# A two-layer decoder trunk on one core: high part of the gated block one flush later, weight-form sums spread behind the residual additions, one activation for the layer 1 operand

## The chip, the cores and the metric

The kernel runs on one core of a Trainium2 chip. The metric is the device time of one execution in microseconds, the median of several runs. Its engines are named as in the profile: PE (matmul) with PEld (weight loads), DVE (vector), ACT (activation), POOL (GpSimd) and SP, which only issues DMAs here.

## The reference, cut to what matters

Two request groups, 1024 prompt positions and 64 sample positions, go through two layers with the same weights. Each layer adds a token mixer (layer 0: convolution and attention; layer 1: short convolution and pooling) and then a gated channel mixer to the residual. The change touches the channel mixers of both layers and the step from layer 0 to layer 1.

```
def rms_norm(x, g):   # x * rsqrt(mean(x*x) + EPS) * g
def swiglu(h, w_in, w_out):
    g, u = jnp.split(h @ w_in, 2, axis=-1)
    return (jax.nn.silu(g) * u) @ w_out
...
for layer in range(DEPTH):                       # DEPTH 2, D_MODEL 1024, FFN_DIM 2816
    hn = rms_norm(h, norm_mix_g[layer])
    ...
    h = h + mix
    h = h + swiglu(rms_norm(h, norm_ffn_g[layer]), w_ffn_in[layer], w_ffn_out[layer])
y = rms_norm(h, norm_final_g)
```

All is float32. A product is made of three matmuls on numbers that are split in a high part (rounded for the PE) and a low part (the rest): high by high, high by low, low by high.

## The kernel before, in words

The residual `hb` lies on chip, transposed: 8 tiles of 128 channels, with 1088 columns for the positions. The columns are worked on as group A (`GA`, 512 columns), group B (`GB`, 576 columns, in two pieces of 288) or both (`GT`, pieces of 364). The order in time is: layer 0 mixers; layer 0 channel mixer of A, with attention in the background; of B; layer 1 mixer for both; layer 1 channel mixer of A; of B with the output.

Weights. `seq` lists the weight blocks in the order in which PE uses them. `w_next()` hands out the next and, before that, prepares the block two places on (`w_split`) and issues loads further on (`w_load`, four `stage` buffers, on SP's queue). To prepare a plain block, ACT copies the high part from `stage` to a tile `hl` (L177) and POOL subtracts to get the low part (L179). There are three `hl` buffers.

The channel mixer (`run_ffn`) has 22 hidden blocks f of 128 channels. Two of them make a group q. After the products of group q+1 come the output products of group q: two weight blocks (o = 0, 1), of four output tiles each (`out_block`, six pieces of matmul per tile and 512 columns), each added to the residual by DVE (`added`, L274). I call these eight output tiles of a group the *out section*, and number them 0 to 7. PE writes results to PSUM accumulators; `accs()` has three buffers in the channel mixers, so output tile 3 needs the addition of tile 0 to be done, tile 4 that of tile 1, and so on.

From f = 5 on, in both groups of layer 1 and in group B of layer 0, the two input products of a block are made with seven half-size products in place of eight (`strassen`). Their weights are four *forms* r = 0 to 3 of a block, of two halves each, built from the two staged halves by four subtractions or additions on DVE: three for form 0 (L186, L187, L188, tile `sum`), one for form 2 or 3 (L191). ACT takes the high part of each half (L194), POOL the low part (L195). In `strassen` PE makes X (two products), Y (two), Z (two), W (one); ACT copies a part of Y (L468), which all of the seven DVE additions (L456) need; the second of these frees X's accumulator, which W takes. The three sums for form 0 of the first block of the next group are issued by the `w_next` of o = 0, at the start of the out section, and so stand on DVE ahead of the additions of the out section.

The gated block. `gated` puts a function `fin` on the list `post`: POOL multiplies (L430), ACT copies the high part to `hid` (L431); the low part (DVE, L432) goes to `late`. `flush()` runs what is on `post` and then what was on `late`; it is called in every plain block, behind X in `strassen`, and behind output tile 1.

Within an engine the instructions run in the order of the program. `tc.manual_schedule()` leaves that order as written.

The step to layer 1 (`to_mixer`) is the last out section of layer 0, group B. For each tile n: the addition, squares (ACT L230, POOL L231), ACT makes the high part of the layer 1 operand `x1` (L351) for B and then for A, and DVE the low parts (L354): that of B one tile later, that of A for all eight tiles behind the whole section.

Of the kernel before, what the change touches and what calls it, by code (L numbers as in the profile page):

```python
# [8 lines left out]
F = mybir.dt.float32  # L9
# [20 lines left out]
def f32(ap):  # L30
    return ap.bitcast(F)
# [27 lines left out]
def trunk_kernel(ctx, tc, x_prompt, x_sample, cache_k, cache_v, state_conformer, state_shortconv, state_pool,  # L59
# [106 lines left out]
    sums = {}  # L166

    def w_split(upto):
        while nxt[1] < min(upto, len(seq)):
            i = nxt[1]  # L170
            w_load(need(i + 1))
            a, b, r = seq[i]
            hl = wpool.tile([128, 2, 1024], FR, name="hl", bufs=3)
            lo, hi = slice(0, 512), slice(512, 1024)
            if b is None:
                st = stage.pop(a)
                act.activation(hl[:, 0], st, AF.Copy)  # L177
                for c in (lo, hi):
                    pool.tensor_tensor(hl[:, 1, c], st[:, c], f32(hl[:, 0, c]), op=OP.subtract)  # L179
                hls[i] = hl.rearrange("p s (k n) -> p s k n", k=loads[a][1])  # L180
            else:
                sg, su = stage[a], stage[b]
                if r == 0:
                    sums["a"], sums["b"] = (sums["p"].tile([128, n], F, name=f"sum{n}") for n in (1024, 512))
                    sa, sb = sums["a"], sums["b"]
                    dve.tensor_tensor(sb[:, lo], su[:, lo], su[:, hi], op=OP.add)  # L186
                    dve.tensor_tensor(sa[:, hi], sg[:, lo], su[:, lo], op=OP.subtract)  # L187
                    dve.tensor_tensor(sa[:, lo], sb[:, lo], sg[:, lo], op=OP.subtract)  # L188
                sa, sb = sums["a"], sums["b"]
                if r == 2:  # L190
                    dve.tensor_tensor(sa[:, hi], sg[:, hi], sa[:, lo], op=OP.subtract)  # L191
                src = ((sa[:, lo], sa[:, hi]), (sb[:, lo], sg[:, lo]), (su[:, hi], sg[:, hi]), (sa[:, hi],))[r]
                for c, x in zip((lo, hi), src):
                    act.activation(hl[:, 0, c], x, AF.Copy)  # L194
                    pool.tensor_tensor(hl[:, 1, c], x, f32(hl[:, 0, c]), op=OP.subtract)  # L195
                if r == 3:
# [83 lines left out]
    def flush():  # L280
        todo, low_parts = post[:], late[:]
        post.clear()
        late.clear()
        for f in todo + low_parts:
            f()
# [63 lines left out]
    def prep(g, x, n, gain, squares=False, c0=0):  # L349
        o, i = x[n][:, :, c0:c0 + g.n], hb[:, n, g.cs]  # L350
# [51 lines left out]
    def run_ffn(g, accs, ps, hidp, x, last, sig=False, slot=lambda: None, forms=None):  # L402
# [21 lines left out]
        def gated(f, t, u):  # L424
# [4 lines left out]
            def fin():  # L429
                pool.tensor_tensor(t[:, :n], t[:, :n], u[:, :n], op=OP.mult)  # L430
                act.activation(dst[:, 0], t[:, :n], AF.Copy)  # L431
                late.append(lambda: dve.tensor_tensor(dst[:, 1], t[:, :n], f32(dst[:, 0]), op=OP.subtract))  # L432
# [52 lines left out]
        for q in range(G + 1):  # L485
# [776 lines left out]
    knew = consts.tile([128, 4, NS], F, name="knew")  # L1262
# [52 lines left out]
    def to_mixer(hh):  # L1315
# [9 lines left out]
        for o in range(2):  # L1325
            h = w_next()
            for i in range(4):
# [399 lines left out]
```

## Time and profile before

| | us |
|---|---|
| median of 3 runs (2681.70 to 2682.96) | 2682.24 |
| the profiled execution | 2677.37 |
| its span, first to last instruction | 2675.2 |
| PE busy in it | 2540.1 (95%) |
| POOL, DVE, ACT busy | 1569.5 (59%), 1637.9 (61%), 1084.8 (41%) |

The mean granted TensorE clock is 0.988. Matmul ends in the trace are modelled, so PE's busy time is an upper figure; the gaps between its instructions and what ended them are what is read below. A row of the wait view says: engine, line, what it waited for, the sum in us, how many times, the longest. A row of the timeline says: start and length in us, engine, line, operation, out<-in, shapes, how many in a row, and in brackets the idle time before it and what ended it.

### The profile page before, as it was taken

The page shows a single profiled execution, that of the slowest core. Times are in us where ns is not written, and L with a number is a line of the kernel's source. Part 1 is how long each engine was busy: PE and PEld are TensorE (multiplying, and loading weights), DVE is VectorE, ACT ScalarE, POOL GpSimd, SP SyncE. Part 2 cuts the span into 40 slices and gives each one's busy share as a digit, 9 for nine tenths or more (in the row PEclk, how much of TensorE's full clock was granted, in tenths as well). Part 3 has the DMA queues.
Part 4 walks back from the last instruction along what each step waited for, and adds up shares of the span by engine and source line. Part 5 has one row for each costly group of instructions (what it writes and reads, how often), then busy time and mean ns, then how long its engine had stood idle before and what let it go on. Part 6 is the DMA issues. An engine that isn't in the chain of part 4 may idle for free. (4 is left out here: it accounts for less than half of the span.)

```text
span 2675.2 us, 40716 instructions
## 1 busy us (share of the span) xinstructions
PE 2540.1 (95%) x15627; PEld 2257.4 (84%) x15627; DVE 1637.9 (61%) x2262; ACT 1084.8 (41%) x1814; POOL 1569.5 (59%) x1199
## 2 busy tenths in 40 slices
PE   8989998999999998999999899999999999999998
PEld 6788877887666656999999899998788888999997
DVE  3774776868756634377666633333666676666665
ACT  5436766744343324343333422122333334333333
POOL 6756244444333337478788722234788887677875
PEclk9999999999999999999999999999999999999999
DMA  7332241234445434322332411131232333233232
GB/s 218 114 97 71 62 112 36 71 112 117 142 142 152 119 110 128 89 72 80 95 95 87 128 44 40 42 113 34 87 93 87 90 95 95 67 104 107 85 90 75
DMA packets 346008, 254.06 MB, mean 95 GB/s; under 512 B 22657, under 2 KB 295169, under 8 KB 345800
## 3 DMA queue, kind: packets, MB, share of 16 engines
q1 hardware_dynamic: 345784, 251.46, 32.1%
q8 instruction: 124, 2.03, 0.3%
q14 instruction: 68, 0.56, 0.1%
q10 hardware_dynamic: 32, 0.01, 0.0%
HBM read 233.21 MB, written 18.69 MB: 94 GB/s over the span
## 5 line engine op out<-in xcount | busy, mean ns | idle before, releaser
L179 POOL TENSOR_TENSOR hl<-stage,hl 128x512 fp32r<-128x512 f32 x484 | 667.6, 1405 | 481.5 <-ACT hl L177 323.7
L214 PE MATMUL acc<-x,hl 128*128 128x288 f32 (+1 forms) x3792 | 710.1, 340 | 12.0 <-DVE hb L274 7.4
L214 PEld LDWEIGHTS acc<-x,hl 128*128 128x128 f32 x3792 | 585.0, 190 | 98.7 <-issue 35.3
L214 PE MATMUL acc<-hid,hl 128*128 128x288 f32 (+1 forms) x3072 | 551.0, 335 | 35.3 <-DVE hb L274 23.6
L214 PEld LDWEIGHTS acc<-hid,hl 128*128 128x128 f32 x3072 | 465.1, 190 | 105.8 <-DVE hb L274 35.1
L274 DVE TENSOR_TENSOR hb<-acc,hb 128x512 f32<-128x512 f32 (+2 forms) x376 | 263.6, 717 | 224.2 <-PE acc L214 222.1
L195 POOL TENSOR_TENSOR hl<-sum,hl 128x512 fp32r<-128x512 f32 x204 | 282.8, 1403 | 172.6 <-ACT hl L194 167.1
L452 PE MATMUL acc<-tt,hl 128*128 128x288 f32 (+1 forms) x2448 | 331.6, 291 | 0.6 <-ACT hl L194 0.3
L452 PEld LDWEIGHTS acc<-tt,hl 128*128 128x128 f32 x2448 | 321.0, 189 | 1.9 <-ACT hl L194 0.6
L177 ACT ACTIVATE hl<-stage 128x1024 fp32r<-128x1024 f32 x242 | 252.0, 1052 | 142.7 <-PE acc L214 100.9
L214 PE MATMUL acc<-x1t,hl 128*128 128x364 f32 (+1 forms) x1728 | 293.8, 331 | 7.4 <-DVE x1t L354 4.1
L214 PEld LDWEIGHTS acc<-x1t,hl 128*128 128x128 f32 x1728 | 288.9, 190 | 9.3 <-DVE x1t L354 4.4
L452 PE MATMUL acc<-x,hl 128*128 128x288 f32 (+1 forms) x1836 | 256.9, 292 | 18.0 <-ACT hl L177 12.9
L456 DVE TENSOR_TENSOR tmp<-acc,tmp 128x288 f32<-128x288 f32 (+1 forms) x357 | 146.5, 442 | 202.7 <-ACT tmp L468 157.9
L452 PEld LDWEIGHTS acc<-x,hl 128*128 128x128 f32 x1836 | 243.8, 190 | 20.8 <-ACT hl L177 19.2
L195 POOL TENSOR_TENSOR hl<-stage,hl 128x512 fp32r<-128x512 f32 x153 | 229.7, 1524 | 20.8 <-ACT hl L194 10.5
L270 DVE TENSOR_TENSOR tmp<-acc,rr 128x512 f32<-128x512 f32 (+3 forms) x128 | 89.7, 712 | 204.7 <-PE acc L214 189.2
L194 ACT ACTIVATE hl<-sum 128x512 fp32r<-128x512 f32 x204 | 122.1, 623 | 186.1 <-DVE sum L188 119.1
L431 ACT ACTIVATE hid<-tmp 128x512 fp32r<-128x512 f32 (+1 forms) x88 | 57.9, 657 | 326.6 <-POOL tmp L430 326.5
L231 POOL TENSOR_TENSOR ss<-ss,tmp 128x512 f32<-128x512 f32 (+2 forms) x62 | 105.2, 1696 | 87.8 <-ACT tmp L230 84.4
L430 POOL TENSOR_TENSOR tmp<-tmp 128x512 f32<-128x512 f32 (+1 forms) x88 | 125.7, 1429 | 26.4 <-ACT tmp L416 25.4
L214 PE MATMUL acc<-x1a,hl 128*128 128x512 f32 x480 | 121.3, 406 | 2.5 <-POOL hl L179 1.3
(252 smaller groups left out, 2936.4 us busy)
## 6 DMA issues: line engine op xcount, KB each, us to landing
stage<-in_w_ffn_in_dram SPq DMA_DIRECT2D x176, 512.0 KB
stage<-in_w_ffn_out_dram SPq DMA_DIRECT2D x88, 512.0 KB
stage<-in_w_in_even_dram SPq DMA_DIRECT2D x40, 512.0 KB
kst<-in_cache_k_dram SPq DMA_DIRECT2D x64, 256.0 KB
vst<-in_cache_v_dram SPq DMA_DIRECT2D x64, 256.0 KB
stage<-in_w_out_even_dram SPq DMA_DIRECT2D x16, 512.0 KB
stage<-in_w_in_odd_dram SPq DMA_DIRECT2D x16, 512.0 KB
park<-hb SPq DMA_DIRECT2D x16, 288.0 KB
```

What stands on the lines that cost most here:

```text
L177: act.activation(hl[:, 0], st, AF.Copy)
L179: pool.tensor_tensor(hl[:, 1, c], st[:, c], f32(hl[:, 0, c]), op=OP.subtract)
L194: act.activation(hl[:, 0, c], x, AF.Copy)
L195: pool.tensor_tensor(hl[:, 1, c], x, f32(hl[:, 0, c]), op=OP.subtract)
L214: pe.matmul(acc[:, b, :c1 - c0], w, x[:, xi, c0:c1], start=first and s == 0, stop=last and s == 2)
L231: pool.tensor_tensor(ss[:, g.cs], ss[:, g.cs], t[:, :g.n], op=OP.add)
L270: dve.tensor_tensor(d, a, r, op=OP.mult)
L274: dve.tensor_tensor(d, a, d, op=OP.add)
L430: pool.tensor_tensor(t[:, :n], t[:, :n], u[:, :n], op=OP.mult)
L431: act.activation(dst[:, 0], t[:, :n], AF.Copy)
L452: pe.matmul(acc[:, :w2], h[:, wi, i, k], xk[:, xi], start=k == 0 and s == 0, stop=k == 3 and s == 2)
L456: dve.tensor_tensor(out, acc[:, :w2], x, op=OP.add)
```

## The change

There are four edits:

1. `fin` has only POOL's multiplication; ACT's high part and DVE's low part are both issued one flush later.
2. In the out section `w_next` runs with `thin` set: the three sums of form 0, and with the third its high and low parts (`cut`), go to `parts_`, and one is run behind each of the additions of output tiles 0, 1 and 2.
3. The fourth sum (form 3) gets a tile of its own, `sum_c`, instead of half of the tile `sum`, and the staged weights are given free at form 2 instead of form 3. `knew` moves from the permanent pool to one that ends with the layer 0 channel mixer of A.
4. In `to_mixer` one activation of 1088 columns makes the high part for both groups; the low parts of A for tiles 0 and 1 are made within the section, the other six behind it.

```diff
@@ w_split
+            a, b, r = seq[i]
             w_load(need(i + 1))
-            a, b, r = seq[i]
...
+                if r == 0:
+                    todo = [lambda: dve.tensor_tensor(sb, su[:, lo], su[:, hi], op=OP.add),
+                            lambda: dve.tensor_tensor(sa[:, hi], sg[:, lo], su[:, lo], op=OP.subtract),
+                            lambda cut=cut: (dve.tensor_tensor(sa[:, lo], sb, sg[:, lo], op=OP.subtract),
+                                     cut(src=(sa[:, lo], sa[:, hi])))]
+                    if thin[0]:
+                        parts_.extend(todo)
+                    else:
+                        for f in todo:
+                            f()
+                else:
+                    while parts_:
+                        parts_.pop(0)()
+                    if r == 2:
+                        sums["c"] = sums["p"].tile([128, 512], F, name="sum_c")
+                        dve.tensor_tensor(sums["c"], sg[:, hi], sa[:, lo], op=OP.subtract)
+                    cut(src=(sb, sg[:, lo]) if r == 1 else (su[:, hi], sg[:, hi]) if r == 2 else (sums["c"],))
                 if r == 2:
...
                     stage.pop(a), stage.pop(b)
@@ gated
                 pool.tensor_tensor(t[:, :n], t[:, :n], u[:, :n], op=OP.mult)
-                act.activation(dst[:, 0], t[:, :n], AF.Copy)
-                late.append(lambda: dve.tensor_tensor(dst[:, 1], t[:, :n], f32(dst[:, 0]), op=OP.subtract))
+                late.append(lambda: split(dst, t[:, :n]))
@@ run_ffn, out section
+                    thin[0] = True
                     h = w_next()
+                    thin[0] = False
                     for i in range(4):
                         a = accs()
                         out_block(g, a, h, i, hh)
                         added(g, hb[:, o * 4 + i, g.cs], a)
+                        if parts_:
+                            parts_.pop(0)()
                         if o == 0 and i == 1:
                             flush()
@@ to_mixer
-                prep(GB, x1, n, pc(MIXG + 8 + n), c0=HALF)
+                gain = pc(MIXG + 8 + n)
+                act.activation(x1[n][:, 0], hb[:, n], AF.Copy, scale=gain)
+                for gr in (GB, GA):
+                    lowq.append(lambda gr=gr, n=n, gain=gain: dve.scalar_tensor_tensor(
+                        x1[n][:, 1, gr.cs], hb[:, n, gr.cs], gain, f32(x1[n][:, 0, gr.cs]), op0=OP.mult,
+                        op1=OP.subtract))
+                if n > 1:
+                    behind.append(lowq.pop())
                 low(1)
-                prep(GA, x1, n, pc(MIXG + 8 + n))
-                behind.append(lowq.pop())
```

ACT, layer 1 channel mixer of group A, from the second `strassen` of a group through the out section, before. `hid` is the gated block, `sum` and `stage` the sources of the forms, L468 the copy out of Y, L177 the two output weight blocks, L481 the silu:

```order
L194 ACTIVATE hl<-stage 128x512 x2
L431 ACTIVATE hid<-tmp 128x512
L194 ACTIVATE hl<-sum_18363 128x512
L468 ACTIVATE tmp<-acc 128x256
L177 ACTIVATE hl<-stage 128x1024 x2
L481 ACTIVATE tmp<-tmp 128x512
L194 ACTIVATE hl<-sum_18551 128x512 x2
L431 ACTIVATE hid<-tmp 128x512
```

The same stretch of ACT now, where the split of `hid` is L231, the forms L189, the copy out of Y L479 and the silu L492:

```order
L189 ACTIVATE hl<-stage 128x512 x2
L189 ACTIVATE hl<-sum_c 128x512
L479 ACTIVATE tmp<-acc 128x256
L177 ACTIVATE hl<-stage 128x1024 x2
L492 ACTIVATE tmp<-tmp 128x512
L231 ACTIVATE hid<-tmp 128x512
L189 ACTIVATE hl<-sum_18566 128x512 x2
```

The copy to `hid` that stood between form 2 and form 3 is gone from there; it now stands in the out section, ahead of form 0.

DVE, the same group, from the second block's additions through the out section, before:

```order
L456 TENSOR_TENSOR tmp<-acc,tmp 128x256 x7
L186 TENSOR_TENSOR sum_20586<-stage 128x512
L187 TENSOR_TENSOR sum_20585<-stage 128x512
L188 TENSOR_TENSOR sum_20585<-sum_20586,stage 128x512
L274 TENSOR_TENSOR hb<-acc,hb 128x512 x2
L432 TENSOR_TENSOR hid<-tmp,hid 128x512
L274 TENSOR_TENSOR hb<-acc,hb 128x512 x6
L191 TENSOR_TENSOR sum_20585<-stage,sum_20585 128x512
```

DVE now, with L286 the residual addition, L193 to L195 the three sums, L232 the low part of `hid`:

```order
L467 TENSOR_TENSOR tmp<-acc,tmp 128x256 x7
L286 TENSOR_TENSOR hb<-acc,hb 128x512
L193 TENSOR_TENSOR sum_20613<-stage 128x512
L286 TENSOR_TENSOR hb<-acc,hb 128x512
L194 TENSOR_TENSOR sum_20612<-stage 128x512
L232 TENSOR_TENSOR hid<-tmp,hid 128x512
L286 TENSOR_TENSOR hb<-acc,hb 128x512
L195 TENSOR_TENSOR sum_20612<-sum_20613,stage 128x512
L286 TENSOR_TENSOR hb<-acc,hb 128x512 x5
L207 TENSOR_TENSOR sum_c<-stage,sum_20612 128x512
```

The first addition now comes ahead of all sums; the third comes behind two sums and the low part.

DVE in the step to layer 1, now; `x1t` is the operand, 576 columns are B and 512 are A. Before, each addition from the third on was followed by one low part of B, and all of A's came at the end:

```order
L286 TENSOR_TENSOR hb<-acc,hb 128x576
L1352 SCALAR_TENSOR_TENSOR x1t_15056<-hb,par,x1t_15056 128x576
L286 TENSOR_TENSOR hb<-acc,hb 128x576
L1352 SCALAR_TENSOR_TENSOR x1t_15056<-hb,par,x1t_15056 128x512
L1352 SCALAR_TENSOR_TENSOR x1t_15057<-hb,par,x1t_15057 128x576
L286 TENSOR_TENSOR hb<-acc,hb 128x576
L1352 SCALAR_TENSOR_TENSOR x1t_15057<-hb,par,x1t_15057 128x512
L286 TENSOR_TENSOR hb<-acc,hb 128x576
L1352 SCALAR_TENSOR_TENSOR x1t_15058<-hb,par,x1t_15058 128x576
```

The low part of B for tile 0 now stands ahead of the second addition, and A's first two low parts stand within the section.

More of the change, by code (lines that the diff above doesn't have):

```diff
@@ L164, in need @@
         return max(a, b or 0) + 1
-    sums = {}
+    sums, parts_, thin = {}, [], [False]
     def w_split(upto):
@@ L280, in flush @@
     def flush():
-        todo, low_parts = post[:], late[:]
+        todo = post + late
         post.clear()
         late.clear()
-        for f in todo + low_parts:
+        for f in todo:
             f()
@@ L1261, in trunk_kernel @@
     hidp = hstack.enter_context(tc.tile_pool(name="hid0", bufs=2, side="right"))
[L1262 removed]
+    knew = hstack.enter_context(tc.tile_pool(name="knewp", bufs=1, side="right")).tile([128, 4, NS], F, name="knew")
     act.activation(knew, kall[:, :, SEQ:T], AF.Copy)
```

20 lines of the change are left out of this document (7 added, 13 removed).

## The prediction

> **What bounds the kernel now.** I read the busy shares first, then who PE waits for by stage, then one period of the steady state engine by engine.
>
> ```profile
> PE 2540.1 (95%) x15627; PEld 2257.4 (84%) x15627; DVE 1637.9 (61%) x2262; ACT 1084.8 (41%) x1814; POOL 1569.5 (59%) x1199
> ```
>
> PE is the bound: 2675.2 of span less 2540.1 leaves 135 us in which it stands, and no edit removes a matmul. So the question is which of PE's waits end at what the edits move. The waits of the stretches with forms, in order: layer 1 group A (1926 to 2226 us), layer 0 group B (1205 to 1500), layer 1 group B (2330 to 2620).
>
> ```profile
> PE acc L452 <- ACT hl L177: 12.9, 9, 2.1
> PE acc L214 <- DVE hb L274: 9.9, 8, 1.3
> ```
> ```profile
> PE acc L214 <- DVE hb L274: 3.3, 8, 0.6
> PE acc L452 <- DVE tmp L456: 3.2, 3, 2.1
> ```
> ```profile
> PE acc L214 <- DVE hb L274: 3.3, 6, 0.7
> PE acc L452 <- DVE tmp L456: 1.6, 1, 1.6
> ```
>
> Two kinds of wait recur: one inside `strassen` (L452), one in the out section (L214 for L274). Here is a period of group A in layer 1: PE, then ACT, DVE, POOL.
>
> ```profile
> 2038.29 1.60 PE L452 MATMUL acc<-x,hl 128*128 128x256 f32 x12
> 2041.24 1.66 PE L452 MATMUL acc<-x,hl 128*128 128x256 f32 x12 [1.36 <-ACT hl L177]
> 2042.74 4.42 PE L214 MATMUL acc<-hid,hl 128*128 128x512 f32 x18
> 2048.39 0.97 PE L214 MATMUL acc<-hid,hl 128*128 128x512 f32 x3 [1.24 <-DVE hb L274]
> ```
> ```profile
> 2038.76 0.63 ACT L431 ACTIVATE hid<-tmp 128x512 fp32r<-128x512 f32 x1 [5.34 <-POOL tmp L430]
> 2039.30 0.61 ACT L194 ACTIVATE hl<-sum 128x512 fp32r<-128x512 f32 x1
> 2039.82 0.37 ACT L468 ACTIVATE tmp<-acc 128x256 f32<-128x256 f32 x1
> 2040.08 2.00 ACT L177 ACTIVATE hl<-stage 128x1024 fp32r<-128x1024 f32 x2
> ```
> ```profile
> 2040.21 2.43 DVE L456 TENSOR_TENSOR tmp<-acc,tmp 128x256 f32<-128x256 f32 x6 [6.40 <-ACT tmp L468]
> 2042.94 0.42 DVE L456 TENSOR_TENSOR tmp<-acc,tmp 128x256 f32<-128x256 f32 x1 [0.30 <-PE acc L452]
> 2043.28 1.06 DVE L186 TENSOR_TENSOR sum<-stage 128x512 f32<-128x512 f32 x1
> 2044.27 1.77 DVE L187 TENSOR_TENSOR sum<-stage 128x512 f32<-128x512 f32 x1
> 2045.96 1.78 DVE L188 TENSOR_TENSOR sum<-sum,stage 128x512 f32<-128x512 f32 x1
> 2047.66 1.27 DVE L274 TENSOR_TENSOR hb<-acc,hb 128x512 f32<-128x512 f32 x2
> 2048.86 1.54 DVE L432 TENSOR_TENSOR hid<-tmp,hid 128x512 fp32r<-128x512 f32 x1
> ```
> ```profile
> 2037.43 1.30 POOL L430 TENSOR_TENSOR tmp<-tmp 128x512 f32<-128x512 f32 x1
> 2039.99 1.27 POOL L195 TENSOR_TENSOR hl<-sum,hl 128x512 fp32r<-128x512 f32 x1 [1.26 <-ACT hl L194]
> 2041.26 5.93 POOL L179 TENSOR_TENSOR hl<-stage,hl 128x512 fp32r<-128x512 f32 x4
> ```
>
> ```profile
> ACT hid L431 <- POOL tmp L430: 326.5, 76, 8.2
> ```
>
> The last row is the sum over the run. The first wait of the period: ACT stands 5.34 us for POOL's multiplication, with L194 and L468 queued behind; DVE stands 6.40 us for L468; its second addition frees X's accumulator at about 2041.1, and PE's W, ready at 2039.9 (2038.29 and 1.60), starts at 2041.24. The row names L177, but L177 is itself behind L431 and L468. The second wait: three tiles take PE from 2042.74 to 2047.16; tile 3 needs the addition of tile 0, which stands behind the three sums and ends at 2048.3.
>
> **The change, part by part.** *A, the copy to hid a flush later.* ACT then meets L431 when its product has long been made. L468 can run when Y is done, just before Z's second product starts at 2038.29; two additions of 0.4 us then free X by about 2039.2, before W is wanted. So the whole 1.36 goes. Eight of the nine waits are such: 12.9 less the longest, 2.1, is 10.8 us. The longest of each stretch (2.1, 2.1, 1.6) is at the first `strassen`, where DVE has other work until shortly before:
>
> ```profile
> 2334.73 1.91 DVE L191 TENSOR_TENSOR sum<-stage,sum 128x512 f32<-128x512 f32 x1
> 2337.72 1.54 DVE L456 TENSOR_TENSOR tmp<-acc,tmp 128x288 f32<-128x288 f32 x3 [1.08 <-ACT tmp L468]
> ```
>
> There only DVE's 1.08 of idleness can be saved: 3 x 1.1 = 3.3. The other two waits of layer 0 (3.2 less 2.1) are 1.1. Together 15.2 us; from below 10 (the steady ones, a little short), from above 17.7 (all of 12.9, 3.2 and 1.6). The delayed copy itself costs nothing inside, since `hid` is read a group later. At the three run ends it stands between the product and DVE's low part; at most 3 x 0.63, and I take 0, since by then eight additions lie between.
>
> *B, sums behind additions.* Nothing is removed: three sums, two or three additions and L432 are the same DVE work in another order. Walk it for group A, with W at 2039.9, so tile 0 at 2041.4 and 1.47 us per tile (4.42/3). The addition of tile 0 (0.69) ends at 2043.8. A sum alone and a sum next to POOL:
>
> ```profile
> 2027.35 0.69 DVE L187 TENSOR_TENSOR sum<-stage 128x512 f32<-128x512 f32 x1 [1.19 <-POOL hl L195]
> ```
>
> 0.69 there, 1.77 above, where POOL ran L179. The first sum meets POOL (L179, then L430): 1.77, to 2045.5; addition 1 to 2046.2; if POOL is done, second sum, L432 and addition 2 take 3 x 0.69, to 2048.3. Tile 3 (2045.8) and tile 4 (2047.3) are then free of waiting, and tile 5 starts at 2048.75, after addition 2. If the second sum meets POOL too, addition 2 ends at 2049.4 and tile 5 waits 0.6; if L432 (1.54 above) does as well, about 1.5, more than the 1.24 before. I take 0.2, near zero, for two reasons: form 3's low part no longer waits 1.26 on POOL, so that its four L179 start earlier, and with `sum_c` the 1.19 before L187 goes too, which brings POOL's earlier parts forward. So 9.9 - 8 x 0.2 = 8.3; bounds -2 and 9.9. In group B a tile takes longer:
>
> ```profile
> 2451.28 4.92 PE L214 MATMUL acc<-hid,hl 128*128 128x288 f32 x36
> 2456.71 8.20 PE L214 MATMUL acc<-hid,hl 128*128 128x288 f32 x60 [0.51 <-DVE hb L274]
> ```
>
> ```profile
> 1531.47 0.75 DVE L274 TENSOR_TENSOR hb<-acc,hb 128x576 f32<-128x576 f32 x1
> ```
>
> The tile takes 1.64 (4.92/3) and its addition 0.75, so tile 5 starts 8.2 after tile 0. DVE there: addition 0 ends at 2.6, then at worst two sums of 1.77, an L432 of 1.54 and two additions of 0.75: 9.2; with one contended, 7.3. I take no wait: 3.3 + 3.3 = 6.6; from below 3. B is 14.9 us. The Trainium skill's page "SBUF — State Buffer" (Who interferes with whom) calls the port that DVE and POOL share a lock for a whole instruction, taken by a DVE operation with two SBUF inputs and blocking the other engine's. By that a sum behind a POOL operation would take 0.69 + 1.30, an estimated 2.0, where the trace has 1.77, and a contended second sum would cost tile 5 another 0.2, so 1.6 us of the sum over eight sections. It speaks against sums between additions, in the direction that the rows show; I keep the rows' 1.77.
>
> *C, the layer 1 operand.* ACT, PE and DVE at the step to layer 1:
>
> ```profile
> 1519.72 1.37 ACT L351 ACTIVATE x1t<-hb,par 128x576 fp32r<-128x576 f32 x2
> 1521.00 0.67 ACT L230 ACTIVATE tmp<-hb 128x576 f32<-128x576 f32 x1
> ```
> ```profile
> 1532.37 0.74 PE L214 MATMUL acc<-x1t,hl 128*128 128x364 f32 x3 [2.88 <-DVE hb L274]
> 1537.17 2.18 PE L214 MATMUL acc<-x1t,hl 128*128 128x364 f32 x6 [4.07 <-DVE x1t L354]
> ```
> ```profile
> 1534.44 10.56 DVE L354 SCALAR_TENSOR_TENSOR x1t<-hb,par,x1t 128x576 fp32r<-128x576 f32 x9 [1.00 <-ACT x1t L351]
> ```
>
> PE waits twice, 6.95 us, and works 0.74 between: for the last addition, then for the first low part of A, behind B's last. The second wait goes, since A's tile 0 is split early. Against that the additions come later: the low part of B for tile 0 now waits for ACT ahead of addition 1, and that of tile 1 ahead of addition 2, which leaves ACT idle twice, an estimated 1.5 each (a low part of some 0.8 and an addition of 0.75). One activation of 1088 columns is worth about 1.1 (one of L177's two above, 1024 columns, takes 1.0), so each tile saves 0.25 of ACT, 7 x 0.25 = 1.8 by the last addition. That puts PE's start at 1532.4 + 3.0 - 1.8 = 1533.6, later by an estimated 0.9 for low parts that meet POOL (1.17 each in the row of nine): 1534.5. It was effectively 1537.17 - 0.74 = 1536.4. I take 1.2 of the 1.9 so got; bounds -1 and 4.
>
> *D, attention in the background, layer 0 group A.* Here the copy of `hid` stands at three places directly ahead of what PE waits for:
>
> ```profile
> 690.08 0.63 ACT L431 ACTIVATE hid<-tmp 128x512 fp32r<-128x512 f32 x1
> ```
>
> It leaves, 3 x 0.6 = 1.8; but it comes back elsewhere in ACT's queue among the attention's copies, where I book the same 1.8 as a cost: 0, bounds -2 and 2. Stages freed one form earlier only let SP's queue issue earlier; SP's order is unchanged and no row above ends at a load: 0. `knew` in another pool: the same instruction, 0.
>
> Sum: 15.2 + 14.9 + 1.2 + 0 = 31.3 us. The profiled execution, 2677.37 (span 2675.2 and 2.2 around it), becomes 2646.1. The median of the runs lies 4.87 above it (2682.24), so 2651.
>
> **Rivals.** *B1: in group A the sums still meet POOL.* All of A and C, and group B's 6.6, but nothing of the 9.9: 23.0, so 2659. For it: the rows of 1.77, and POOL is the second busiest there:
>
> ```profile
> 1960.00:1994.50 34.50, 31.89 (x218) 29.07 (x217) 22.83 (x32) 12.56 (x22) 28.50 (x20) 1.00 0.32 91
> ```
>
> Of 34.5 us PE has 31.89 and POOL 28.50. Against it: POOL has only L430 to do between the four L179 and the low parts of form 0, which now come behind the third sum. *B2: W is held by something else* (the row says L177). Then A is lost: 31.3 - 15.2 = 16.1, 2666. Against it: L177 and L468 both stand behind the same 5.34. *B3: no measurable change*, 2682: the waits are an artefact of modelled matmul ends. Against it: eight waits of one size (9.9 in all, the longest 1.3) with one releaser. *B4, slower: form 0 comes too late.* If POOL works through the whole out section, every sum is 1.77 and L432 1.54: in A tile 5 waits 1.5 and, as form 0's two low parts end 2.6 us of POOL later, the next X waits some 0.7; in B tiles 5 and 6 wait 1.0 and 0.9. That is 8 x 2.2 + 16 x 1.9 = 48 us of new waits, against 31.3: 17 slower, 2699. It decides from 31.3/24 = 1.3 us of new wait per section. For it: DVE's work is not less. Against it: the POOL rows above.
>
> **How the numbers follow.** My forecast, 2643 to 2656: 0.55. B1, 2656 to 2663: 0.2. B2 and other part losses, to 2676: 0.14. B3: 0.06. B4 or another new wait: 0.05. Below 0.2% (5.4 us) a run cannot be told from no change. Faster 0.89, same 0.06, slower 0.05. The low end is all bounds at their best, 17.7 + 16.5 + 4 + 2 = 40, 2642; I take 2643. The high end takes in B1 and B2 with a margin: 2669. Its parts hold some 0.83.
>
> **What would show it.** A: the wait L452 for L177 is gone from layer 1 group A, and ACT's 326 us of waiting of `hid` for POOL, over the run, is mostly gone. B: L214's wait for the addition moves from tile 3 to tile 5 or vanishes; the period falls from 34.5 to about 32. C: one wait of PE before `x1t` in place of two. I would be wrong if the period of group A stayed above 33.5, if PE waited for L190 or L189 at X (form 0 late), or if a low part of `x1t` held additions so long that PE started it after 1536.

## The result, and the profile after

The median of the changed kernel is 2653.38 us (4 runs, 2651.86 to 2657.19) against 2681.97 for the kernel before on the same chip (4 runs, 2675.75 to 2682.96): a ratio of 0.990, interval 0.988 to 0.992, or 28.6 us less. The forecast was 2651. The profiled executions say less than the medians: 2677.37 before, which is low among its runs, and 2657.19 after, the highest of its runs, 20.2 apart.

The busy line after:

```profile
PE 2544.4 (96%) x15627; PEld 2263.9 (85%) x15627; DVE 1622.3 (61%) x2262; ACT 1085.1 (41%) x1806; POOL 1553.1 (58%) x1199
```

PE does the same 15627 matmuls and stands 111 us (2655.4 of span less 2544.4) in place of 135. Who it waits for, in the same three stretches as before the change (layer 1 group A; layer 0 group B; layer 1 group B). `strassen`'s matmul is now L463, the output tile's L226, the addition L286:

```profile
PE acc L226 <- DVE hb L286: 4.7, 4, 3.8
PE acc L463 <- DVE tmp L467: 3.1, 7, 0.4
PE acc L463 <- ACT hl L177: 1.8, 1, 1.8
PE acc L226 <- DVE hid L232: 0.5, 1, 0.5
```
```profile
PE acc L463 <- DVE tmp L467: 1.7, 1, 1.7
```
```profile
PE acc L463 <- DVE tmp L467: 1.6, 1, 1.6
PE acc L463 <- ACT hl L189: 0.5, 1, 0.5
```

Both kinds of wait that the forecast spoke of look spent: 12.9, 3.2 and 1.6 inside `strassen` became 4.9, 1.7 and 1.6, and of 9.9, 3.3 and 3.3 for the additions 0.9 is left beside one new wait of 3.8. Read alone, this says that A gave some 9 us and B some 15. The runs below show that this reading is wrong.

To see where each run's time goes, the trace is cut where PE's norm matmuls (those on `ones`) start a stage. In us, one profiled execution each:

| | L0 group A and attention | L0 group B | L1 mixers | L1 group A | L1 group B | median of its runs |
|---|---|---|---|---|---|---|
| before | 677.7 | 426.1 | 301.2 | 393.6 | 408.6 | 2681.97 |
| A alone | 678.9 | 418.4 | 301.2 | 380.4 | 404.3 | 2652.74 |
| B alone | 682.2 | 422.2 | 301.2 | 386.2 | 402.6 | 2668.50 |
| changed kernel | 678.8 | 418.0 | 301.1 | 385.9 | 403.3 | 2653.38 |
| changed, A taken back | 682.3 | 422.1 | 301.2 | 384.8 | 403.2 | 2663.65 |
| changed, B taken back | 678.7 | 418.5 | 301.2 | 379.4 | 403.4 | 2652.34 |

A part of these differences is the clock and not the edit. In all 14 traces PE's granted clock falls at times to 0.5, for 3.4 us or longer, and each fall begins while PE waits or less than 2 us behind a wait. One in the changed kernel, at the wait of 3.76 us that ends at 2205.63 (a row says: window, its length, PE busy and matmuls, granted clock, share and GB/s of DMA):

```profile
2194.00:2203.90 9.90, 7.86 (x37) 1.00 0.60 177
2203.90:2210.70 6.80, 5.07 (x12) 0.50 0.27 78
2210.70:2220.00 9.30, 8.85 (x37) 1.00 0.20 58
```

Matmuls of 512 columns start 0.43 us apart in it and 0.23 behind it, so the 12 of them cost an estimated 2.4 us on top of the wait. In layer 1 group A of the changed kernel PE waits 17.8 us behind the norm, less than in A alone (20.0) or with B taken back (19.3), and the stage is still 5.5 and 6.5 us longer: PE stands at half clock for 20.5 us there and for 10.2 in each of the other two.

### The profile page after: what moved, and what is told of

Read it like the earlier page. It is cut to its first block, busy times and chain, and to the rows that moved or that the text cites. A ratio compares the mean times of both kernels' runs of the same rounds, so it can differ in the third digit from the quotient of the medians.

```text
span 2655.4 us, 40689 instructions
## 1 busy us (share of the span) xinstructions
PE 2544.4 (96%) x15627; PEld 2263.9 (85%) x15627; DVE 1622.3 (61%) x2262; ACT 1085.1 (41%) x1806; POOL 1553.1 (58%) x1199
## 5 line engine op out<-in xcount | busy, mean ns | idle before, releaser
L179 POOL TENSOR_TENSOR hl<-stage,hl 128x512 fp32r<-128x512 f32 x484 | 656.3, 1379 | 485.7 <-ACT hl L177 334.3
L226 PE MATMUL acc<-x,hl 128*128 128x288 f32 (+1 forms) x3792 | 709.8, 340 | 11.8 <-DVE hb L286 7.9
L226 PEld LDWEIGHTS acc<-x,hl 128*128 128x128 f32 x3792 | 585.0, 190 | 98.1 <-issue 38.4
L226 PE MATMUL acc<-hid,hl 128*128 128x288 f32 (+1 forms) x3072 | 554.1, 337 | 26.3 <-DVE tmp L282 13.8
L226 PEld LDWEIGHTS acc<-hid,hl 128*128 128x128 f32 x3072 | 470.1, 191 | 94.4 <-DVE hb L286 15.9
L286 DVE TENSOR_TENSOR hb<-acc,hb 128x512 f32<-128x512 f32 (+2 forms) x376 | 266.7, 718 | 245.8 <-PE acc L226 244.5
L177 ACT ACTIVATE hl<-stage 128x1024 fp32r<-128x1024 f32 x242 | 253.5, 1053 | 213.5 <-PE acc L226 136.8
L463 PE MATMUL acc<-tt,hl 128*128 128x288 f32 (+1 forms) x2448 | 331.6, 291 | 0.5 <-ACT hl L189 0.5
L463 PEld LDWEIGHTS acc<-tt,hl 128*128 128x128 f32 x2448 | 321.0, 189 | 1.7 <-ACT hl L189 0.7
L226 PE MATMUL acc<-x1t,hl 128*128 128x364 f32 (+1 forms) x1728 | 294.7, 332 | 5.5 <-DVE hb L286 5.0
L226 PEld LDWEIGHTS acc<-x1t,hl 128*128 128x128 f32 x1728 | 290.2, 191 | 7.1 <-ACT x1t L1350 5.2
L190 POOL TENSOR_TENSOR hl<-sum,hl 128x512 fp32r<-128x512 f32 x153 | 199.1, 1328 | 158.6 <-ACT hl L189 158.6
L463 PE MATMUL acc<-x,hl 128*128 128x288 f32 (+1 forms) x1836 | 257.1, 292 | 8.3 <-DVE tmp L467 6.5
L463 PEld LDWEIGHTS acc<-x,hl 128*128 128x128 f32 x1836 | 243.8, 190 | 11.2 <-ACT hl L177 5.7
L190 POOL TENSOR_TENSOR hl<-stage,hl 128x512 fp32r<-128x512 f32 x153 | 227.5, 1509 | 18.8 <-ACT hl L189 18.8
L189 ACT ACTIVATE hl<-sum 128x512 fp32r<-128x512 f32 x153 | 87.6, 624 | 209.3 <-DVE sum L195 190.6
L232 DVE TENSOR_TENSOR hid<-tmp,hid 128x512 fp32r<-128x512 f32 (+1 forms) x88 | 95.7, 1087 | 56.4 <-ACT hid L231 56.0
L226 PE MATMUL acc<-x1a,hl 128*128 128x512 f32 x480 | 122.1, 408 | 3.0 <-POOL hl L179 1.3
```

Of the source, the lines that this page charges most:

```text
L226: pe.matmul(acc[:, b, :c1 - c0], w, x[:, xi, c0:c1], start=first and s == 0, stop=last and s == 2)
L232: dve.tensor_tensor(dst[:, 1], src, f32(dst[:, 0]), op=OP.subtract)
L286: dve.tensor_tensor(d, a, d, op=OP.add)
L463: pe.matmul(acc[:, :w2], h[:, wi, i, k], xk[:, xi], start=k == 0 and s == 0, stop=k == 3 and s == 2)
```

## The experiments

**One part taken back at a time.**

A taken back (`gated`; a block of code shows the lines that differ, and `...` stands for lines left out):

```
-                late.append(lambda: split(dst, t[:, :n]))
+                act.activation(dst[:, 0], t[:, :n], AF.Copy)
+                late.append(lambda: dve.tensor_tensor(dst[:, 1], t[:, :n], f32(dst[:, 0]), op=OP.subtract))
```

> The changed kernel with part A alone taken back: the high part of the gated block is copied by ACT in the same flush as POOL's multiplication, as before; sums behind additions, sum_c and the layer 1 operand stay. My theory, from the waits of the two profiles: the nine waits inside the first products after the output sections of layer 1 group A go back from 5.0 to 12.9 us, the first of layer 0 group B from 1.7 to 3.2, and against that the 6.5 us of waits around 1889 to 1898 us go back to the 4.1 of before: some 7 us slower than the changed kernel, 2660. Should the new 3.76 us wait at 2205.6 us be A's too, 2656. Rival 1, the forecast's own size of A, 15.2: 2668.5. Rival 2, with the sums spread A is worth nothing, since DVE is then busy where it stood idle: 2653.

Measured: 2663.65 us (ratio to before 0.993, 0.992 to 0.995), 10.3 slower than the changed kernel. In layer 1 group A the wait inside `strassen` is back in full, and the 0.45 that the spread sums cause stays beside it (the line numbers are this kernel's):

```profile
PE acc L464 <- ACT hl L177: 12.8, 9, 2.1
PE acc L464 <- DVE tmp L468: 3.6, 8, 0.5
```

B taken back (the output sections):

```
-                    thin[0] = True
```

> The changed kernel with part B alone taken back: all three sums for form 0 stand ahead of the additions of the output section again; the copy a flush later, sum_c and the layer 1 operand stay. My theory, from the waits of the two profiles: the waits of the output tiles for their additions come back (9.9 in layer 1 group A, 3.3 and 3.3 in the two groups B, now 0.9 in all): 15.6 us slower than the changed kernel, 2669, with a wait of about 1.2 us at output tile 3 of every section of layer 1 group A. Rival: most of these 15.6 are A's or sum_c's doing (POOL's work has moved too, so that the sums would now run free of it at 0.69 each instead of 1.06, 1.77 and 1.77, 2.5 us sooner per section), so that the waits at tile 3 stay away in group A: 2653 to 2657.

Measured: 2652.34 us (0.990, 0.989 to 0.992): no slower. My theory fell, and the rival's reason with it: the waits for the additions did come back in group A, and nothing came of it. In layer 1 group A:

```profile
PE acc L226 <- DVE hb L286: 10.2, 8, 1.4
PE acc L463 <- POOL hl L190: 0.9, 2, 0.6
```

So 10.2 us of waits at output tile 3 stand here against the 4.7, 3.1 and 1.8 of the changed kernel. One price of B shows when both are laid side by side. The third sum for the next block's form 0 (L195) and the additions behind it, in the changed kernel (DVE, POOL, then PE):

```profile
2046.12 1.78 DVE L193 TENSOR_TENSOR sum<-stage 128x512 f32<-128x512 f32 x1
2049.53 1.78 DVE L195 TENSOR_TENSOR sum<-sum,stage 128x512 f32<-128x512 f32 x1
2051.23 2.39 DVE L467 TENSOR_TENSOR tmp<-acc,tmp 128x256 f32<-128x256 f32 x6
```
```profile
2043.85 5.21 POOL L190 TENSOR_TENSOR hl<-stage,hl 128x512 fp32r<-128x512 f32 x3
2049.02 1.74 POOL L190 TENSOR_TENSOR hl<-sum_c,hl 128x512 fp32r<-128x512 f32 x1
```
```profile
2050.20 1.60 PE L463 MATMUL acc<-x,hl 128*128 128x256 f32 x12
2052.25 0.95 PE L463 MATMUL acc<-x,hl 128*128 128x256 f32 x6 [0.45 <-DVE tmp L467]
```

and with B taken back, in the corresponding period:

```profile
2013.66 1.78 DVE L193 TENSOR_TENSOR sum<-stage 128x512 f32<-128x512 f32 x1
2017.06 0.68 DVE L195 TENSOR_TENSOR sum<-sum,stage 128x512 f32<-128x512 f32 x1
2017.66 2.47 DVE L467 TENSOR_TENSOR tmp<-acc,tmp 128x256 f32<-128x256 f32 x6
```
```profile
2014.85 1.74 POOL L190 TENSOR_TENSOR hl<-sum_c,hl 128x512 fp32r<-128x512 f32 x1
```
```profile
2017.73 3.04 PE L463 MATMUL acc<-x,hl 128*128 128x256 f32 x24
```

Sums behind additions end later, so POOL's low parts of forms 0 to 3 start later: from L193, its last one (`sum_c`) begins 2.90 us on (2049.02 less 2046.12) in place of 1.19, so that it meets the third sum, which takes 1.78 for 0.68. The additions start 5.11 us behind L193's start in place of 4.00, and W waits. W was due at 2051.64 (12 matmuls are 1.44 apart; the row's 1.60 is a modelled end) and starts at 2052.25: 0.61 lost, of which the row shows 0.45. With B taken back, the 24 matmuls of Z's second product and W run through.

C taken back (`to_mixer`):

```
-                act.activation(x1[n][:, 0], hb[:, n], AF.Copy, scale=gain)
...
+                prep(GB, x1, n, pc(MIXG + 8 + n), c0=HALF)
+                low(1)
+                prep(GA, x1, n, pc(MIXG + 8 + n))
+                behind.append(lowq.pop())
```

> The changed kernel with part C alone taken back: the layer 1 operand in two high parts, the low part of B one tile later and that of A behind the section. My theory: PE waits twice again at the step to layer 1, 2.9 and 4.1 us (6.95 in all) in place of 1.36 and 5.03: 0.6 us slower, 2654, too small for the time to tell, so that the two waits in the trace decide. Rival, the forecast: 1.2 us slower. Rival 2: the additions that now wait for ACT cost more than the second wait, so that taking C back is 1 us or more faster.

Measured: 2654.31 us (0.990, 0.988 to 0.991), within what can be told apart. In place of the changed kernel's one wait ahead of the operand's first matmuls and a new one of 1.36 inside the section, the two waits of before are back: 2.87 and 3.56, 6.43 in all (first two rows), against 1.36 and 5.03, 6.39 in all (last two). By the medians C is worth 0.9 us, which cannot be told from nothing.

```profile
1531.71 1.25 PE L226 MATMUL acc<-x1t,hl 128*128 128x364 f32 x3 [2.87 <-DVE hb L286]
1536.52 3.69 PE L226 MATMUL acc<-x1t,hl 128*128 128x364 f32 x11 [3.56 <-DVE x1t L366]
```
```profile
1518.30 5.43 PE L226 MATMUL acc<-hid,hl 128*128 128x288 f32 x36 [1.36 <-DVE hb L286]
1528.76 3.67 PE L226 MATMUL acc<-x1t,hl 128*128 128x364 f32 x11 [5.03 <-DVE hb L286]
```

`sum_c` taken back:

```
-                        sums["c"] = sums["p"].tile([128, 512], F, name="sum_c")
-                        dve.tensor_tensor(sums["c"], sg[:, hi], sa[:, lo], op=OP.subtract)
+                        dve.tensor_tensor(sa[:, hi], sg[:, hi], sa[:, lo], op=OP.subtract)
```

> The changed kernel with the sum of form 3 written over the second half of the first sum again, as before, in place of a tile of its own (sum_c), so that DVE waits there for POOL to have read it. My theory: the 0.45 us for which PE waits in each first product after an output section, seven times in layer 1 group A, comes from the sums of the next form meeting POOL's low parts, since DVE no longer waits for POOL; with the wait back the waits inside these products vanish (3.2 us) and nothing else on PE appears: 3 us faster, 2650, and no wait of PE for L456's successor there. Rival: the 0.45 stays, and the wait of DVE for POOL holds the additions that free the accumulators: 1.2 us more in each of some 25 groups, slower by up to 8 us at PE's slack: 2654 to 2661.

Measured: 2651.41 us (0.989, 0.988 to 0.991), 2 less than the changed kernel with overlapping intervals: no difference that can be told. But the trace decides against my theory of the 0.45: it is 0.77 to 0.78 here, eight times (6.2 us). `sum_c` does not cause the meeting of sum and low part; it shortens it.

**One part alone on the kernel before.** A alone:

```
-                act.activation(dst[:, 0], t[:, :n], AF.Copy)
-                late.append(lambda: dve.tensor_tensor(dst[:, 1], t[:, :n], f32(dst[:, 0]), op=OP.subtract))
+                late.append(lambda: split(dst, t[:, :n]))
```

> The kernel before with part A alone: ACT copies the high part of the gated block a flush later; sums ahead of the additions, no sum_c, the operand of layer 1 as before. My theory, that A carries nearly the whole gain and the spread sums nothing on top of it: 2652 to 2655, with the waits of PE for L214's addition at output tile 3 still there in layer 1 group A (1.2 each, 9.9 in all) and gone or halved in both groups B. Rival: sum_c, which stayed when the spread sums were taken back, did part of it (POOL's low parts start earlier): then 2660 to 2666, the forecast's 15.2 for A alone.

Measured: 2652.74 us (0.990, 0.988 to 0.991). A alone is the whole gain. In layer 1 group A its waits for the additions are the largest of all, 10.9 us; in the two groups B (layer 0, then layer 1) they are nearly gone, from 3.3 and 3.3, though no sum was moved:

```profile
PE acc L214 <- DVE hb L274: 10.9, 8, 1.4
```
```profile
PE acc L214 <- DVE hb L274: 1.3, 2, 0.8
```
```profile
PE acc L214 <- DVE hb L274: 0.6, 1, 0.6
```

Why in group B: POOL. Layer 1 group B before (POOL, DVE):

```profile
2448.05 1.30 POOL L195 TENSOR_TENSOR hl<-sum,hl 128x512 fp32r<-128x512 f32 x1 [1.32 <-ACT hl L194]
2449.35 5.49 POOL L179 TENSOR_TENSOR hl<-stage,hl 128x512 fp32r<-128x512 f32 x4
```
```profile
2451.86 1.83 DVE L186 TENSOR_TENSOR sum<-stage 128x512 f32<-128x512 f32 x1
2455.91 1.41 DVE L274 TENSOR_TENSOR hb<-acc,hb 128x576 f32<-128x576 f32 x2
```

and with A alone (POOL, DVE, PE):

```profile
2426.05 1.29 POOL L195 TENSOR_TENSOR hl<-sum,hl 128x512 fp32r<-128x512 f32 x1
2430.41 2.99 POOL L179 TENSOR_TENSOR hl<-stage,hl 128x512 fp32r<-128x512 f32 x2 [0.38 <-ACT hl L177]
```
```profile
2431.20 1.05 DVE L186 TENSOR_TENSOR sum<-stage 128x512 f32<-128x512 f32 x1
2434.47 1.41 DVE L274 TENSOR_TENSOR hb<-acc,hb 128x576 f32<-128x576 f32 x2
```
```profile
2430.62 12.85 PE L214 MATMUL acc<-hid,hl 128*128 128x288 f32 x96
```

Before, form 3's low part waits 1.32 for ACT, which stands at L431; POOL is through with the four L179 at 2454.84, 3.56 after output tile 0 starts at 2451.28. With A alone this wait is gone, POOL is through 2.78 after tile 0 starts (2433.40 less 2430.62), the first sum takes 1.05 for 1.83, and the additions start 3.85 after tile 0 in place of 4.63: in time for tile 3, so that PE runs 96 matmuls without a stop.

B alone: the diff of the change without its `fin`, its `sum_c` and its `to_mixer`.

> The kernel before with part B alone, without sum_c: the sums behind additions 0, 1, 2; the copy of the high part and the layer 1 operand as before. My theory: as with A taken back from the changed kernel (2663.65), some 17 us faster than before, 2664 to 2666; the tile-3 waits gone (15.6) and the waits inside the products of half size in layer 1 group A as before, 12.9. Rival: sum_c is needed for it (DVE's wait for POOL ahead of the sums comes back and pushes them): 2670 or more.

Measured: 2668.50 us (0.996, 0.994 to 0.997): B alone gains 13, some 5 less than with `sum_c` and C beside it (2663.65). In layer 1 group A both kinds of wait stand inside `strassen`:

```profile
PE acc L463 <- ACT hl L177: 12.8, 9, 2.1
PE acc L463 <- DVE tmp L467: 6.2, 8, 0.8
```

**What the changed kernel still loses.** The third sum behind the second addition (which frees the accumulator for W), in `strassen` only:

```
+            thin[0] = 1                # w_next() leaves the third sum on parts_
             Z, h = accs(), w_next()
+            thin[0] = 0
...
             add(U[:, b], X[:, 1], U[:, a])
+            while parts_:
+                parts_.pop(0)()
```

> The changed kernel with one sum moved: in a block of half-size products, the third of the three sums for the next block's form 0, which meets POOL's low part of sum_c (1.78 us where it takes 0.68 with part B taken back), stands behind the second addition, which frees the accumulator that W takes, in place of ahead of the first. My theory, that the spread sums gave back inside these products what they saved in the output section: the seven 0.45 us waits (0.61 us with what the row hides) and most of the first 1.83 vanish from layer 1 group A, and as the third sum then runs when POOL is through with sum_c it ends no later than before: 5 to 6 us faster, 2648. Rival: form 0 of the next block comes later by the length of the sum, PE waits at the next X instead (a new wait for L190 of 0.5 to 1 us per group): 2653 to 2658.

Measured: 2649.45 us (0.989, 0.987 to 0.990), 3.9 less than the changed kernel by the medians, with overlapping intervals. W no longer waits, and a part of the rival holds: the second block's X does, for form 0's low part, 0.3 at a time. The third sum (0.99) between additions, PE's Z and W, PE's next X (4.79 where 36 such matmuls take 4.48), and this kernel's waits in layer 1 group A:

```profile
2045.35 0.99 DVE L195 TENSOR_TENSOR sum<-sum,stage 128x512 f32<-128x512 f32 x1
```
```profile
2045.24 3.04 PE L465 MATMUL acc<-x,hl 128*128 128x256 f32 x24
2048.12 4.79 PE L465 MATMUL acc<-tt,hl 128*128 128x256 f32 x36
```
```profile
PE acc L228 <- DVE hb L288: 4.4, 3, 3.8
PE acc L465 <- POOL hl L190: 3.0, 10, 0.6
```

The flush of a run's last output section behind tile 5 in place of tile 1:

```
-                        if o == 0 and i == 1:
+                        if i == 1 and o == (1 if forms and q == G - 1 else 0):
```

> The changed kernel with one flush moved: in the last output section of a run with forms it stands behind output tile 5 in place of tile 1, so that DVE's low part of the gated block comes when POOL has done its weights. My theory: the 3.76 us wait of PE at 2205.6 us came of DVE's low part (6.66 us long beside five POOL operations back to back) ahead of an addition; it shrinks to under 0.7, and the profiled execution gets some 3 us shorter; since the long low part is not seen in every execution (the trace without the sums' spreading had none there), the median gains 0 to 3: 2650 to 2653. Rival: the addition there waits for something else (PSUM, a late matmul), and a wait over 3 us stays at that place.

Measured: 2652.58 us (0.990, 0.988 to 0.991), the same within the intervals; but the wait it aimed at is gone. DVE and PE at the place in the changed kernel, and DVE with the flush late:

```profile
2198.31 6.66 DVE L232 TENSOR_TENSOR hid<-tmp,hid 128x512 fp32r<-128x512 f32 x1
```
```profile
2205.63 7.70 PE L226 MATMUL acc<-hid,hl 128*128 128x512 f32 x22 [3.76 <-DVE hb L286]
```
```profile
2204.20 0.97 DVE L232 TENSOR_TENSOR hid<-tmp,hid 128x512 fp32r<-128x512 f32 x1
```

Its layer 1 group A takes 376.6 us where the changed kernel's took 385.9: PE waits 5.0 us less there and stands at half clock for 10.2 us in place of 20.5. Its layer 0 group A, whose code the edit leaves as it is, takes 683.1 us in this execution for 678.8, so the profile shows a gain that the median does not. The next two look at the plain blocks, layer 0's above all.

A only in blocks of half-size products; the plain blocks copy as before:

```
+                if forms and f >= PLAIN:
                     late.append(lambda: split(dst, t[:, :n]))
+                else:
+                    act.activation(dst[:, 0], t[:, :n], AF.Copy)
+                    late.append(...)       # the low part, as before
```

> The changed kernel with the later copy of the gated block's high part only in blocks of half-size products; in the plain blocks ACT copies it in the flush of POOL's multiplication, as before. My theory: with the later copy, DVE's low part in a plain block waits for ACT's copy in the same flush, which stands behind ACT's other work, and the reading of PSUM (L282) waits behind it: 3.7 us (8.7 in two other runs) at the end of layer 0 group A, 6.5 at 1889 to 1898 us, 4.46 at 2288; with the copy earlier these become 0.6, 2.8 and 3.6, while the wait near 1180 us gets 1.6 longer: some 6 us faster, 2647, up to 10 if the long wait of layer 0 is the usual one. Rival: the waits stay, since POOL's multiplication is what ACT, then DVE, wait for: 2653 or more.

Measured: 2660.43 us (0.992, 0.991 to 0.993), 7 slower than the changed kernel (one of its six runs took 2651.56, the others 2659.11 to 2661.50): the theory fell. At the places it named the waits did shrink (2.0 at the end of layer 0 group A; 1.3, 0.45 and 1.45 where there were 6.5). But the stretch of layer 0 group A with attention in the background (from its norm to the next) takes 547.2 us in place of 543.0, both with 13.7 us at half clock, and layer 0 group B 421.8 in place of 418.0. So the later copy is worth some 7 us in the plain blocks of layer 0 (682.2 less 678.8 up to the norm of group B, and 3.8 in group B), for which the forecast booked 0. The five kernels that copy early there have 542.7 to 547.2 in that stretch, and those that copy late throughout 540 to 543. The 542.7 is the profiled execution of before, with 3.4 us at half clock; the other four have 10.2 to 13.7 us of it and 545.8 or more.

The three edits together:

> The three moves of the flush, the third sum and the later copy in blocks of half-size products only, together, on the changed kernel. If they add up: 6 for the copy, 5 for the sum, 0 to 3 for the flush, 11 to 14 us: 2640 to 2642. Rival: they free the same time twice, as the later copy and the spread sums seem to have done (each taken back alone gave 10 and 0 us, both together 28): 2645 to 2648.

Measured: 2652.42 us (0.990, 0.989 to 0.991). Late flush and third sum are worth 8 us on top of the copy edit (2660.43), which takes them away again: the time is that of the changed kernel. Then the first two, with the early copy in layer 1's plain blocks only (`lag` is False there):

```
-                if forms and f >= PLAIN:
+                if lag or f >= PLAIN:
```

> The changed kernel with the late flush and the moved third sum, and the gated block's copy in the same flush as POOL's multiplication in the plain blocks of layer 1 alone. My theory, from the traces of the runs before: the third sum alone gave 2649.45; in its trace the late flush takes 3.75 and 0.45 us at 2200 to 2208, and the copy takes the waits of 6.5 at 1886 to 1895 to 3.2 and 4.46 at 2283 to 3.64, while layer 0 keeps the later copy, which taking it back in the plain blocks showed to be worth some 7 us: 2641 to 2643. Rival: a low part that POOL holds off for several operations turns up at the end of layer 0 group A (a wait of 8.7 us there in three traces, 3.7 in the others) and takes 5 of it: 2646 to 2648.

Measured: 2647.91 us (0.988, 0.986 to 0.989; single runs 2643.57 to 2655.97). The rival came: the long low part at the end of layer 0 group A. It is there in four of the traces (C back, `sum_c` back, flush late, this one), 5.72 us each time; in the changed kernel the same instruction took 0.71. With C taken back the code of that stage is the changed kernel's, so it comes and goes without an edit there. First DVE and PE with C taken back, then DVE in the changed kernel:

```profile
1041.66 5.72 DVE L232 TENSOR_TENSOR hid<-tmp,hid 128x512 fp32r<-128x512 f32 x1 [9.91 <-ACT hid L231]
```
```profile
1048.04 1.22 PE L226 MATMUL acc<-hid,hl 128*128 128x512 f32 x2 [8.69 <-DVE tmp L282]
```
```profile
1041.95 0.71 DVE L232 TENSOR_TENSOR hid<-tmp,hid 128x512 fp32r<-128x512 f32 x1 [9.96 <-ACT hid L231]
```

Of the 9.9 us ahead of it a part is A's doing: the copy (L231) is now in the flush of the low part and stands behind ACT's other copies, and with the early copy these are 5.57 us (A taken back) and 6.50 (before). Last, the copy early also in the last two blocks of layer 0 group A:

```
-                if lag or f >= PLAIN:
+                if (lag and f < NF - 2) or (forms and f >= PLAIN):
```

> As the run with the late flush, the moved third sum and the early copy in layer 1's plain blocks (2647.9, executions from 2643.6 to 2656.0), and the early copy also for the last two hidden blocks of layer 0 group A. My theory: DVE's low part at the end of that stretch, 5.72 us long beside five POOL operations in four of the traces, holds PSUM's reading and costs PE 8.69 us there (3.7 where it is not held so long); with the copy a flush earlier it is issued before POOL's run of operations and PE waits 2.0: 1.7 to 6.6 faster, 2642 to 2646, and the trace shows no low part over 3.2 us. Rival: the early copy stands in front of the attention's copies on ACT, and what it saves at the end is lost in the stretch before (as where all plain blocks had it, 547 us in place of 540 to 543): 2648 to 2652.

Measured: 2647.57 us (0.988, 0.986 to 0.990). In its trace PE waits 0.61 at the end of that stage, no low part of the gated block is over 2.0, and from the norm of layer 0 group A to that of group B it takes 675.7 us, without the rival's loss; the run with the third sum moved, which copies late there and met no long low part, also took 675.7. The median is no lower than the run before it, whose spread shows that not every execution has the long low part. The last two are the fastest versions tried, 5.5 and 5.8 us below the changed kernel by the medians; the intervals still overlap.

## Why the prediction was right, and where it was not

The time was right (2653.4 for 2651) by luck: its division was wrong, and A gave about as much more than forecast as B gave less.

- **A, 15.2 forecast, 28.9 measured alone.** The direction and the mechanism inside `strassen` were right: the wait for L431 is gone, and layer 1 group A gains 13.2 us. By stages, 13.2, 7.7 and 4.3 (layer 1 group A and the two groups B, A alone against before, with the same time at half clock) and 3.3 in layer 0 group A (B alone, which copies early, less A alone) come to 28.5. The term was mis-sized in three places. First, 1.36 was the row's idle time behind a modelled end; W started 1.51 after it was due (2041.24 less 2038.29 and 1.44), and the period fell by about as much. Second, group B: the step put the tile-3 waits, 6.6, under B, but they hang on POOL's start, which A moves: 7.7 and 4.3 us less in the two groups B, some 3.8 of the 7.7 in plain blocks. Third, D booked 0 for layer 0 group A; the run that copies early in plain blocks was 7 us slower, some half of it there and half in the plain blocks of layer 0 group B. That the 2.1, 2.1 and 1.6 at the first `strassen` of each run would lose 1.1 each did not come true in group B (1.7 and 1.6 left). And that the delayed copy "costs nothing inside" failed in the plain blocks of layer 1 group A: PE waits 6.5 us there in place of the 4.7 of before (3.8 where only the half-size blocks copy late).
- **B, 14.9 forecast, nothing on top of A.** The walk over the output section was right: the tile waits vanish. The walk stopped there. It left out that form 0 and with it POOL's low parts end later, so that POOL meets the sums of the *next* block. The rival B4 named the late low parts but looked for the wait at X; it is at W. In layer 1 group A the period is 33.04 us with A alone (1969.58 to 2167.81, six of them) and 32.70 in the changed kernel (1986.58 to 2182.81): 0.34 left of the 1.39 of the tile wait. In the profiled execution that (8 x 0.34 = 2.7) is more than spent on the 3.76 at 2205 us, the late first W (1.83 for 0.61) and the 6.8 and 3.4 us at half clock that came with them. The 3.76 is there in all four kernels with A in the half-size blocks, B, `sum_c` and the flush behind tile 1, the late first W is not: with C taken back, where the channel mixer's code is the same, PE waits 0.61. Moving the flush ends the 3.76 without moving the median, so how much of B's loss each of these is in the usual execution stays open.
- **C, 1.2 forecast, 0.9 measured**, within the noise; the waits' sum hardly moved.
- **D, 0 forecast with bounds of 2**: outside them, see A.
- **The offset of 4.87 us** from profiled execution to median was carried over as if it were fixed. After, the profiled execution lies 3.8 above the median. Before's profiled execution has 542.7 us in the attention stretch where the others with the early copy have 545.8 to 547.2. The clock accounts for that: 3.4 us at half clock against 10.2 to 13.7, an estimated 3.4 to 5.1 us. So the offset was one execution's luck with the clock, as far as one stretch shows it; no other execution of it has a trace.

What I had named as signs, the row for L177 gone from group A and a period below 33.5, A alone shows as well, so they could not tell the forecast's division from another; in the changed kernel that row is not quite gone (1.8, once). Of the signs of being wrong one came, without weight: PE waited once for L189 at X, 0.5 us in layer 1 group B. Only taking parts away showed the division.

## What to carry to other kernels

Two waits in one period on one chain of engines are not two gains: when A makes DVE and POOL earlier, it pays for B's wait too, so forecast each part alone and then the second given the first. Follow a moved piece of work to the engine that consumes it and one block further, since the wait that vanishes in one section can come back at the next buffer. After a good result, take each part out once before believing the waits. And before a difference of a few us between two traces is put down to an edit, compare how long PE's clock was halved in that stage.

## What the runs showed of the hardware that was not expected

A DVE operation with two inputs in SBUF beside a POOL that works without a pause does not always wait for one POOL operation. The low part of 0.69 us took 6.66 at 2198.31 and 6.64 to 6.65 in three other kernels at that place, always across five POOL operations, and it ended only 0.55 after the last of them; here are POOL's, back to back:

```profile
2193.18 7.55 POOL L179 TENSOR_TENSOR hl<-stage,hl 128x512 fp32r<-128x512 f32 x6
2200.69 1.29 POOL L442 TENSOR_TENSOR tmp<-tmp 128x512 f32<-128x512 f32 x1
2201.95 2.47 POOL L179 TENSOR_TENSOR hl<-stage,hl 128x512 fp32r<-128x512 f32 x2
```

The sum behind addition 0 takes 3.10 to 3.11 in three sections of layer 1 group A, across three POOL operations, and 1.53 to 1.86 in the others. Additions with one input in PSUM took 0.69 beside the same POOL operations. In the kernel before, the same low part beside the same six L179 took 1.70; what decides between 1.70 and 6.66 stays open. The Trainium skill's page "SBUF — State Buffer" (Who interferes with whom) calls the port pair that DVE and POOL share an exclusive lock, and has a DVE instruction with two SBUF inputs contend with a POOL instruction that reads SBUF. A DVE operation of 0.69 that waits out one POOL operation of 1.29 would take an estimated 1.98 by that. The trace stays below it where DVE waits for one (1.70 above) and goes beyond it here, as if POOL got the port again each time while DVE waited.

A wait of PE can cost more than its length. All 196 stretches at half clock in the 14 traces begin during a wait of PE or at most 1.84 us behind one, and every wait over 3.2 us, but for the one that each kernel starts with, has such a stretch; the waits of 1.36 us in layer 1 group A of the kernel before have none. With B taken back one begins behind a wait of 0.80 us (at 1014.5 us), so the length of a wait by itself does not decide; what does stays open.
